# A ten-stage block kernel: work at the stage boundaries moved token tile by token tile

## The chip, the cores and the metric

The kernel runs on one core of a Trainium2 chip as one launch. The metric is the device time of one execution in microseconds (us), as the median of the runs made; lower is better. Names of engines as the profile has them: PE is the tensor engine's matmul stream, PEld its weight loads, DVE the vector engine, ACT the scalar engine, POOL GpSimd, SP the engine whose queue issues the DMAs.

## The reference, cut to what matters

256 tokens of width 1024 pass through two layers of a first block (a mixer of four branches, then a feed-forward network) and two layers of a second block (a mixer, an attention over 256 memory tokens, then a dense feed-forward network in layer 0 and eight experts with top 2 in layer 1). Every stage has the same skeleton:

```python
h = rms_norm(x, gain)
...
x = x + rms_norm(f @ w_out, gain_post)
```

In the first block the stage's output is normed before it is added; in the second it is added plainly (`x = x + f @ w_out`). All is float32. `h` feeds the next projections, all of them with K = 1024: `h @ w_in` and the like.

## The kernel before

Ten stages run one after the other: mix1, ffn1, mix1, ffn1, mix2, mem, ffn2 (dense), mix2, mem, ffn2 (`moe`). `xt` holds x as two token tiles of 128 rows, each in two halves of 512 columns. A float32 product is made of three matmuls in float32r (`mm3`, L310 to L312): each operand is split into a high part and a rest, so that a weight tile costs an ACT copy (L297) and a DVE subtraction (L298) after its DMA, all in `wload`. `wload` has 3 buffers for what the DMA brings (`wraw`, 512 KB each) and 4 for the split weights (`wsp`).

A stage ends with `as_1024` (L481): token-major `x @ W`, granule after granule of 128 rows of W, into four PSUM banks `po[t][n]`. The last granules (`TM` = 3 of 8 for mix1, `TF` = 4 of 22 for the ffns) have split weights of their own and are gone through bank by bank: all of token tile 0's two banks, then those of tile 1. What is left of the update of x is put in `pend` by `post_norm` (first block) or `add_x` (second block).

The next stage begins with `norm_T` (L364). It runs the pending update and the norm in the order of a string: `p` squares an output half, `g` multiplies by the gain, `r` makes the scale of the row (a DVE add, a POOL power), `u` updates x, `q` squares it, `s` makes the scale, `n` scales the row into `xn`; the digits are token tile and half. For this stretch the order of ACT and DVE is the one written out (`manual_schedule`); elsewhere a planner orders the instructions of an engine, and puts them where its model of times finds them ready. Then PE makes 16 transposes of `xn`, and ACT (`hh`, L333) and DVE (`hl`, L334) split the eight feature tiles, both token tiles together, with the gain column applied. `late` holds back the fourth weight load of the next stage until that is done; the first three may go before. Only then does the first projection start: in the ffn with weights as the stationary operand and 256 tokens moving (`ws_bank`); in mix1 with `w1a`, in mix2 with `pk` (keys, 200 columns), then `pi` (index queries, 512 columns).

In mix2 the order of PE is written out. It is `pk`'s matmuls, `pi`'s, the transposes of `keys` (L1012 to L1016), `pq`'s, and so on:

```python
pk = as_512(A['w2k'][l], h, 2, 200, "pk2")
pi = as_512(A['w2i'][l], h, 4, 512, "pq2")
keys(pk)
pq = as_512(A['w2q'][l], h, 4, 512, "pq2")
```

`keys` takes the two banks of `pk` (one for each token tile) through an rms scale per head and the rotary turn on ACT, DVE and POOL, tile 0 and then tile 1, and then has PE transpose the result `kd`.

In mix1 a string `SC1` gives PE's order, one letter a step of a generator (`v` is the gate's projection and its gelu). `moe` begins with the router's matmuls on `hh`, `hl` (L1656); it also needs the normed rows token-major with the gain (`th`), which POOL makes by four products with a gain row (L1701).

Of the kernel before, what the change touches and what calls it, by code (L numbers as in the profile page):

```python
# [9 lines left out]
F32 = mybir.dt.float32  # L10
# [48 lines left out]
# ---------------------------------------------------------------- host layout  # L59
# [13 lines left out]
PFM_W = _o  # L73

# [63 lines left out]
def pack(inp):  # L138
    z = {k: np.asarray(v) for k, v in inp.items()}
    d = {}  # L140
# [18 lines left out]
    d['pfm'] = np.stack(pf)  # L159

    a1, c1, s1, g1, u1, v1, gt, uq, ukv, ob, ou, fi, fo = [[] for _ in range(13)]
    for l in range(2):
# [19 lines left out]
        fi.append(_ws(h, 128))  # L182
        fo.append(_as(z['w_ffn_out'][l], 1))
    for nme, v in (('w1a', a1), ('w1c', c1), ('w1s', s1), ('w1u', u1), ('w1v', v1), ('w1g', gt), ('wuq', uq),
                   ('wukv', ukv), ('wob', ob), ('wou', ou), ('wfi', fi), ('wfo', fo)):
        d[nme] = np.stack(v)
# [32 lines left out]
    d['wf2'] = _ws(np.stack([gw, uw], 2).reshape(1024, 5632), 128)  # L219
# [9 lines left out]
    d['ffn2row'] = z['norm_ffn_2'][1:2]  # L229
# [3 lines left out]
# ---------------------------------------------------------------- device  # L233
def build(tc, A, out, stages=None, dbg=None):
# [3 lines left out]
    with ctx:  # L238
        mk = lambda n, b, **k: ctx.enter_context(tc.tile_pool(name=n, bufs=b, **k))
        cp = mk("cp", 1)  # L240
        wraw = mk("wraw", 3)
        wsp = mk("wsp", 4)
        hp = mk("hp", 1)
        st = mk("st", 6)
        scr = mk("scr", 3)
# [19 lines left out]
        # ------------------------------------------------ constants  # L265
# [21 lines left out]
        # ------------------------------------------------ helpers  # L287
# [29 lines left out]
        def ws_tile(o, w, x, kt, nt=0):  # L317
            """o [128, 256] = W[:, nt]^T x; w = (h, l) [128, kt, n]."""
# [26 lines left out]
        def mean_rstd(s2):  # L345
            """s2: the mean square of a row in two parts."""
# [8 lines left out]
        def settle():  # L355
            """what is left of the last update of xt, where no norm of its rows follows at once."""
# [7 lines left out]
        def norm_T(xs, gcol, pl=None, name="h"):  # L364
            """feature-major rms-normalised rows of xs, in two float32r parts; token-major.
            A pending update of xs is made in step with it."""
            pl = pl or hp
            u = pend.pop() if pend else dict(step={}, order='q00 q01 s0 n00 n01 q10 q11 s1 n10 n11', xn=None, close=lambda: None)
            hh = pl.tile([128, 8, 256], F32R, name=name + "h", tag="hh")
            hl = pl.tile([128, 8, 256], F32R, name=name + "l", tag="hl")  # L370
            xn = u['xn'] or hp.tile([128, 2, 1024], F32, name="xn", tag="x8")
# [1481 lines left out]
```

## Time and profile before

| what | before |
|---|---|
| runs, us | 2417.47, 2415.18, 2412.37; median 2415.18 |
| profiled execution, span from first to last instruction | 2401.5 us |
| median of the runs less that span | 13.7 us |
| PE busy | 2298.4 us, 96% of the span |
| DVE, ACT, POOL busy | 72%, 53%, 8% |
| mean granted PE clock | 0.977 of full speed |
| DMA | 429 MB, mean 179 GB/s |

The profiled execution's own time is its span; what the runs show beyond it lies around the program. A matmul's listed duration overlaps the next one's, so the cost of a stream is read from the distance of its starts, not from durations. Idle time of an engine that nothing waits for costs nothing.

### The profile page before, as it was taken

The page shows a single profiled execution, that of the slowest core. Times are in us where ns is not written, and L with a number is a line of the kernel's source. Part 1 is how long each engine was busy: PE and PEld are TensorE (multiplying, and loading weights), DVE is VectorE, ACT ScalarE, POOL GpSimd, SP SyncE. Part 2 cuts the span into 40 slices and gives each one's busy share as a digit, 9 for nine tenths or more (in the row PEclk, how much of TensorE's full clock was granted, in tenths as well). Part 3 has the DMA queues.
Part 4 walks back from the last instruction along what each step waited for, and adds up shares of the span by engine and source line. Part 5 has one row for each costly group of instructions (what it writes and reads, how often), then busy time and mean ns, then how long its engine had stood idle before and what let it go on. Part 6 is the DMA issues. An engine that isn't in the chain of part 4 may idle for free.

```text
span 2401.5 us, 39006 instructions
## 1 busy us (share of the span) xinstructions
PE 2298.4 (96%) x15116; PEld 2060.5 (86%) x15116; DVE 1732.2 (72%) x2879; ACT 1274.9 (53%) x1991; POOL 185.2 (8%) x179
## 2 busy tenths in 40 slices
PE   7999999999999999999999999999999979999998
PEld 7999989979999899787798799888788768888886
DVE  7987665559967655586946655477865768999987
ACT  5544454445544544456324554456432657777775
POOL 0100200001001100001111100001111110000000
PEclk9999999999999999999989999999998989999999
DMA  6455655645456565643214445553212548888986
GB/s 203 132 160 177 180 174 183 185 153 167 143 174 185 165 185 178 191 136 125 75 43 144 146 151 184 190 171 114 96 45 83 198 158 287 321 321 322 345 326 234
DMA packets 123218, 429.24 MB, mean 179 GB/s; under 512 B 14189, under 2 KB 15213, under 8 KB 123025
## 3 DMA queue, kind: packets, MB, share of 16 engines
q1 hardware_dynamic: 123024, 426.68, 54.6%
q8 instruction: 120, 1.97, 0.3%
q14 instruction: 74, 0.60, 0.1%
HBM read 425.57 MB, written 1.05 MB: 178 GB/s over the span
## 4 chain that ended last, share of the span: by engine, by line
PE 75%; DVE 9%; ACT 4%; DMA 3%; POOL 2%; issue 2%; POOLq 0%; ACTq 0%; DVEq 0%
PE pf L311 5%; PE pf L312 5%; PE pf L310 5%; PE pg L310 4%; PE pg L311 4%; PE pg L312 4%; PE po L312 3%; PE po L310 3%; PE po L311 3%; PE pgu L311 3%; PE pgu L312 3%; PE pgu L310 3%; DVE wl L298 2%; PE py L310 1%; PE pb L310 1%
## 5 line engine op out<-in xcount | busy, mean ns | idle before, releaser
L298 DVE TENSOR_TENSOR wl<-raw,wh 128x1024 fp32r<-128x1024 f32 (+2 forms) x788 | 947.7, 1214 | 323.5 <-ACT wh L297 315.3
L297 ACT ACTIVATE wh<-raw 128x1024 fp32r<-128x1024 f32 (+2 forms) x788 | 807.0, 1031 | 609.1 <-PE pg L311 137.5
L311 PE MATMUL pf<-hl,wh 128*128 128x256 f32 x1056 | 299.4, 284 | 0.3
L312 PE MATMUL pf<-hh,wl 128*128 128x256 f32 x1056 | 298.8, 283 | 0.0
L310 PE MATMUL pf<-hh,wh 128*128 128x256 f32 x1056 | 298.7, 284 | 0.0
L310 PE MATMUL pg<-hh,wh 128*128 128x256 f32 x768 | 225.6, 294 | 0.1
L312 PE MATMUL pg<-hh,wl 128*128 128x256 f32 x768 | 220.4, 287 | 1.0 <-DVE wl L298 1.0
L311 PE MATMUL pg<-hl,wh 128*128 128x256 f32 x768 | 220.4, 287 | 0.0
L311 PEld LDWEIGHTS pf<-hl,wh 128*128 128x128 f32 x1056 | 202.7, 192 | 1.3 <-DVE hl L334 1.3
L312 PEld LDWEIGHTS pf<-hh,wl 128*128 128x128 f32 x1056 | 202.7, 192 | 0.0
L310 PEld LDWEIGHTS pf<-hh,wh 128*128 128x128 f32 x1056 | 202.5, 192 | 0.2
L310 PEld LDWEIGHTS pg<-hh,wh 128*128 128x128 f32 x768 | 150.8, 196 | 4.9 <-issue 3.7
L311 PEld LDWEIGHTS pg<-hl,wh 128*128 128x128 f32 x768 | 150.9, 196 | 1.1 <-issue 1.0
L312 PEld LDWEIGHTS pg<-hh,wl 128*128 128x128 f32 x768 | 150.5, 196 | 1.4 <-DVE wl L298 1.4
L311 PE MATMUL pgu<-wl,heh 128*128 128x512 f32 (+1 forms) x384 | 145.3, 378 | 2.0 <-DVE wl L298 2.0
L312 PE MATMUL pgu<-wh,hel 128*128 128x512 f32 (+1 forms) x384 | 144.1, 375 | 0.0
L310 PE MATMUL pgu<-wh,heh 128*128 128x512 f32 (+1 forms) x384 | 143.4, 376 | 0.0
L566 DVE SCALAR_TENSOR_TENSOR yc<-z,htap,yc 128x256 f32<-128x256 f32 x240 | 110.7, 487 | 2.3
L310 PE MATMUL po<-wh,fh 128*128 128x512 f32 x216 | 85.7, 397 | 0.0
L311 PE MATMUL po<-wl,fh 128*128 128x512 f32 x216 | 85.4, 395 | 0.0
L312 PE MATMUL po<-wh,fl 128*128 128x512 f32 x216 | 85.4, 395 | 0.0
L311 PEld LDWEIGHTS pgu<-wl,heh 128*128 128x128 f32 x384 | 72.5, 189 | 13.9 <-DVE wl L298 3.1
(678 smaller groups left out, 5254.3 us busy)
## 6 DMA issues: line engine op xcount, KB each, us to landing
raw<-in_xg_dram SPq DMA_DIRECT2D x128, 512.0 KB, 5.4
raw<-in_wfi_dram SPq DMA_DIRECT2D x88, 512.0 KB, 3.6
raw<-in_xd_dram SPq DMA_DIRECT2D x88, 512.0 KB, 5.2
raw<-in_w1g_dram SPq DMA_DIRECT2D x64, 512.0 KB, 3.6
raw<-in_xg_dram SPq DMA_DIRECT2D x64, 384.0 KB, 4.6
raw<-in_wfo_dram SPq DMA_DIRECT2D x44, 512.0 KB, 3.7
raw<-in_wf_dram SPq DMA_DIRECT2D x44, 512.0 KB, 3.6
raw<-in_wob_dram SPq DMA_DIRECT2D x32, 512.0 KB, 3.7
```

The source lines that it names most:

```text
L297: act.activation(h[:, :n], r[:, :n], AF.Copy)
L298: dve.tensor_tensor(l[:, :n], r[:, :n], h[:, :n].bitcast(F32), op=OP.subtract)
L310: pe.matmul(o, a[0], b[0], start=first, stop=False)
L311: pe.matmul(o, a[0], b[1], start=False, stop=False)
L312: pe.matmul(o, a[1], b[0], start=False, stop=last)
L566: bg.append(lambda z=z, f=f, tap=tap, k=k: dve.scalar_tensor_tensor(yc[:, f], z[:, k:k + 256], tap, yc[:, f], op0=OP.mult, op1=OP.add))
```

## The change

What it does, in ten parts.

- The tails of `as_1024` become longer: `TF` 4 to 6, `TM` 3 to 5. In mix1 the split weights of the tail take tiles that are free by then.
- `norm_T` stays for the memory tokens; for x it is replaced by `norm_x`. The gain is a row, loaded one stage ahead (`gload`), and multiplied in with the scale: `n` is now a SCALAR_TENSOR_TENSOR. The order strings go on through the transposes (`T`), the high parts (`h`), the rests (`l`) and a first projection (`F`), each for one token tile, and PE is in the written order too. With no update pending (`ONEW`) only PE's order is written.
- `head` loads four granules of a 512-column weight ahead of the norm, so before its ACT and DVE steps, and gives `F`: 24 matmuls of 512 columns for one token tile, tokens stationary.
- What `F` is: in mix1 `v`'s projection, in the three dense ffns the first 512 columns (two gate and two up tiles; then 4 transposes bring the result feature-major), in mix2 `pi`. `mem` and `moe` have no `F`.
- In mix2 `pi` therefore goes ahead of `pk`, and nothing stands between `pk` and `keys` any more.
- `late` now holds back the first weight load behind the head's (the fourth for `mem` and `moe`).
- `SC1` is changed: `v` first, and the `u` steps earlier.
- `moe` takes `th` straight from `xn`; POOL's four products and the row's load are gone. `th` now lies in the buffers of `hh` and `hl`.
- `mh` of mix1 moves to other buffers; the pools are allocated from both ends of SBUF.
- Comments and docstrings are gone.

```diff
-OPOST = 'p00 g00 p01 g01 r0 p10 g10 p11 u00 q00 r1 u01 g11 q01 u10 q10 s0 u11 q11 n00 n01 s1 n10 n11'
-OADD = 'u00 q00 u01 q01 s0 u10 q10 n00 u11 n01 q11 s1 n10 n11'
-TF, TM, TE = 4, 3, 4
+OPOST = ('p00 g00 p01 r0 g01 u00 q00 u01 q01 g10 s0 p10 n00 n01 T0 h00 l00 p11 r1 h01 l01 g11 F0 '
+         'u10 q10 u11 q11 s1 n10 n11 T1 h10 l10 h11 l11 F1')
+OADD = ('u00 q00 u01 q01 s0 u10 n00 n01 T0 h00 l00 h01 l01 F0 '
+        'q10 u11 q11 s1 n10 n11 T1 h10 l10 h11 l11 F1')
+ONEW = 'q00 q01 s0 n00 n01 T0 h00 l00 h01 l01 F0 q10 q11 s1 n10 n11 T1 h10 l10 h11 l11 F1'
+TF, TM, TE = 6, 5, 4
-SC1 = ('ccckcchhchhhhhhvxvxvvacssassaxxssasassaassusuuuurggguggagggg'
+SC1 = ('vccckcchhchhhhhsxsxssacssassaxxuuasuauuaassusrgggggagggg'
...
+        def gload(l, n):
+            gains.append(cp.tile([128, 1024], F32, name="gn", tag="gn"))
+            nc.sync.dma_start(gains[-1], A['gnorm'][l, GN.index(n):GN.index(n) + 1].to_broadcast([128, 1024]))
+        def norm_x(first=None, free=0):
...
+            def scale(t, n):
+                dve.scalar_tensor_tensor(xn[:, t, HALF[n]], xt[:, t, HALF[n]], rs[t], gn[:, HALF[n]], op0=OP.mult, op1=OP.mult)
+            def turn(t):
+                for n in range(2):
+                    p = pT[t, n] = psum("pT")
+                    for k in range(4):
+                        c = slice(k * 128, (k + 1) * 128)
+                        pe.transpose(p[:, c], xn[:, t, n * 512 + k * 128:n * 512 + (k + 1) * 128], ident)
...
+            def high(t, n):
+                ins['a'] = act.activation(part(hh, t, n), quad(pT[t, n]), AF.Copy)
+            def low(t, n):
+                ins['d'] = dve.tensor_tensor(part(hl, t, n), quad(pT[t, n]), part(hh, t, n).bitcast(F32), op=OP.subtract)
+            step = dict(u['step'], q=square, s=stat, n=scale, T=turn, h=high, l=low,
+                        F=(lambda t: first(t, (hh, hl))) if first else lambda t: None)
+            with tc.manual_schedule(engines={E_.Activation, E_.DVE, E_.PE} if u['step'] else {E_.PE}):
+                for c_ in u['order'].split():
+                    step[c_[0]](*map(int, c_[1:]))
...
+            if u['step']:
+                late.extend([None] * free + [(ins['a'].ins, ins['d'].ins)])
+        def head(srcs, n, kt, nm):
+            ws = [sub3(wload(src, kt * n), kt) for src in srcs]
+            pz = []
+            def part(t, h):
+                pz.append(pmm(nm)[:, :n])
+                c = slice(t * 128, (t + 1) * 128)
+                for k in range(8):
+                    w = ws[k // kt]
+                    mm3(pz[t], (h[0][:, k, c], h[1][:, k, c]), (w[0][:, k % kt], w[1][:, k % kt]), k == 0, k == 7)
+            return part, pz
...
         def mix1(l):
-            h = norm_T(xt, G(l, 'mixpre'))
+            fv, pzv = head([A['w1v'][l, g] for g in range(4)], 512, 2, "pgv")
+            h = norm_x(fv)
...
-        def ffn_core(wi, wo, h, nt):
+        def ffn_core(wa, wi, wo, nt, ahead):
+            ff, pz = head([wa[g] for g in range(4)], 512, 2, "pfa")
+            h = norm_x(ff)
...
         def mix2(l):
-            h = norm_T(xt, G(l, 'mix2'))
+            fi_, pi = head([A['w2i'][l, g] for g in range(4)], 512, 2, "pq2")
+            h = norm_x(fi_)
...
                 pk = as_512(A['w2k'][l], h, 2, 200, "pk2")
-                pi = as_512(A['w2i'][l], h, 4, 512, "pq2")
                 keys(pk)
                 pq = as_512(A['w2q'][l], h, 4, 512, "pq2")
...
-                moe(h)
+                moe(norm_x(free=3))
...
-                th = [xp.tile([128, 2, 1024], F32R, name="th" + c_) for c_ in "hl"]
+                th = [hp.tile([128, 2, 1024], F32R, name="th" + c_, tag="h" + c_) for c_ in "hl"]
...
-                        pool.tensor_tensor(d, d, grow[:, ns], op=OP.mult)
```

## Rows read from the trace of the kernel before

**Rows 1.** Page, part 1: engine busy us, share of the span, instructions.

```profile
PE 2298.4 (96%) x15116; PEld 2060.5 (86%) x15116; DVE 1732.2 (72%) x2879; ACT 1274.9 (53%) x1991; POOL 185.2 (8%) x179
```

**Rows 2.** PE's waits, whole span: who waited for whom, us, times, longest.

```profile
PE pT L393 <- DVE pn L383: 20.1, 5, 5.2
PE pT L393 <- DVE xn L383: 14.1, 9, 7.8
...
PE pS L633 <- DVE yal L332: 3.1, 2, 1.6
```

**Rows 3.** PE's timeline, first mix1 to ffn1: start, duration, instruction, idle before.

```profile
313.83 0.40 PE L311 MATMUL po<-wtl,mh 128*128 128x512 f32 x1
314.07 0.40 PE L312 MATMUL po<-wth,ml 128*128 128x512 f32 x1
319.66 3.70 PE L393 MATMUL pT<-cst,pn 128*128 128x128 f32 x16 [5.20 <-DVE pn L383]
```

**Rows 4.** Windows, that ffn's `pf` matmuls alone: busy, count, clock, DMA.

```profile
322.00:336.00 14.00, 12.94 (x104) 0.95 0.35 114
322.00:340.00 18.00, 16.94 (x137) 0.96 0.45 130
```

**Rows 5.** Windows of PE at two boundaries: busy (count), granted clock, DMA share, GB/s.

```profile
316.00:318.00 2.00, 0.00 (x0) 0.63 0.08 31
322.00:323.00 1.00, 1.00 (x7) 0.50 0.00 0
323.00:324.00 1.00, 1.00 (x9) 0.83 0.00 0
1580.00:1582.00 2.00, 2.00 (x12) 0.50 0.49 107
```

**Rows 6.** Groups by form, 291 to 340 us: steps of the norm (busy, mean ns).

```profile
L350 POOL TENSOR_TENSOR r<-v,mhalf 128x1 f32<-128x1 f32 x4 | 3.0, 745 | 19.1 <-DVE v L348 19.1
L465 DVE SCALAR_TENSOR_TENSOR xt<-pn,r,xt 128x512 f32<-128x512 f32 x4 | 3.0, 744 | 0.1
L458 DVE TENSOR_TENSOR pn<-po,grow 128x512 f32<-128x512 f32 x4 | 2.6, 681 | 0.0
```

**Rows 7.** ACT's timeline in the tail of the first ffn1: the weight splits.

```profile
489.90 1.06 ACT L297 ACTIVATE wh<-raw 128x1024 fp32r<-128x1024 f32 x1 [1.74 <-PE po L312]
490.93 1.06 ACT L297 ACTIVATE wth<-raw 128x1024 fp32r<-128x1024 f32 x1
493.93 1.06 ACT L297 ACTIVATE wth<-raw 128x1024 fp32r<-128x1024 f32 x1 [1.94 <-DMA raw<-in_wfo_dram]
```

**Rows 8.** Timeline, first mix2: `pk`'s last matmul, the chain of `keys`, its transposes.

```profile
1028.63 0.28 PE L312 MATMUL pk<-wh,hl 128*128 128x200 f32 x1
...
1031.99 0.23 DVE L1009 COPY kd<-kd 128x128 f32<-128x128 f32 x1
...
1035.37 1.22 DVE L298 TENSOR_TENSOR wl<-raw,wh 128x1024 fp32r<-128x1024 f32 x1
...
1036.89 0.23 DVE L1009 COPY kd<-kd 128x128 f32<-128x128 f32 x1
...
1039.68 0.60 PE L1015 MATMUL pT<-cst,kd 128*128 128x128 f32 x4
```

**Rows 9.** PE's waits, mem to ffn2 (1350 to 1420), ffn2 to mix2 (1560 to 1620).

```profile
PE pT L393 <- DVE xn L383: 1.9, 3, 1.2
...
PE pT L393 <- DVE xn L383: 2.0, 2, 1.2
```

**Rows 10.** PE's timeline, beginning of `moe`.

```profile
1945.76 1.09 PE L393 MATMUL pT<-cst,xn 128*128 128x128 f32 x8 [1.18 <-DVE xn L383]
1948.46 0.39 PE L1656 MATMUL plT<-hh,w 128*16 128x256 f32 x1 [1.60 <-DVE hl L334]
...
1957.51 0.58 PE L1707 MATMUL pps<-sel,cst 128*128 128x16 f32 x2 [4.58 <-DVE w L1689]
```

**Rows 11.** PE's timeline, first stage: its first projection.

```profile
12.47 0.62 PE L310 MATMUL pz<-wh,hh 128*128 128x272 f32 x2
```

More of the change, by code (lines that the diff above doesn't have):

```diff
@@ L159, in pack @@
     d['pfm'] = np.stack(pf)
-    a1, c1, s1, g1, u1, v1, gt, uq, ukv, ob, ou, fi, fo = [[] for _ in range(13)]
+    d['gnorm'] = np.stack([z[n] for n in GN], 1)
+    a1, c1, s1, g1, u1, v1, gt, uq, ukv, ob, ou, fi, fo, fa = [[] for _ in range(14)]
+    first = lambda w: _as(w[:, :512].reshape(1024, 2, 2, 128).transpose(0, 2, 1, 3).reshape(1024, 512), 2)
     for l in range(2):
@@ L362, in settle, with norm_T @@
                 u['close']()
-        def norm_T(xs, gcol, pl=None, name="h"):
-            pl = pl or hp
-            u = pend.pop() if pend else dict(step={}, order='q00 q01 s0 n00 n01 q10 q11 s1 n10 n11', xn=None, close=lambda: None)
+        def norm_T(xs, gcol, pl, name):
             hh = pl.tile([128, 8, 256], F32R, name=name + "h", tag="hh")
             hl = pl.tile([128, 8, 256], F32R, name=name + "l", tag="hl")
+            xn = hp.tile([128, 2, 1024], F32, name="xn", tag="x8")
+            s2 = [tiny(2, "s2") for t in range(2)]
+            for t in range(2):
+                for n in range(2):
+                    d = scr.tile([128, 512], F32, name="sq", tag="s512")
+                    act.activation(d, xs[:, t, HALF[n]], AF.Square, scale=1.0 / 32, accum_out=s2[t][:, n:n + 1])
+                r = mean_rstd(s2[t])
+                for n in range(2):
+                    dve.tensor_scalar(xn[:, t, HALF[n]], xs[:, t, HALF[n]], r, None, op0=OP.mult)
+            ps_ = [bank2("pT") for k2 in range(4)]
+            with tc.manual_schedule(engines={mybir.EngineType.PE}):
+                for k in range(8):
+                    for t in range(2):
+                        pe.transpose(ps_[k // 2][:, k % 2, t * 128:(t + 1) * 128], xn[:, t, k * 128:(k + 1) * 128], ident)
+            for k in range(8):
+                split(hh[:, k], hl[:, k], ps_[k // 2][:, k % 2], gcol[:, k:k + 1])
+            return hh, hl
@@ new lines, in build @@
+        gains = []
+        def gload(l, n):
+            gains.append(cp.tile([128, 1024], F32, name="gn", tag="gn"))
+            nc.sync.dma_start(gains[-1], A['gnorm'][l, GN.index(n):GN.index(n) + 1].to_broadcast([128, 1024]))
+        def norm_x(first=None, free=0):
+            u = pend.pop() if pend else dict(step={}, order=ONEW, xn=None, close=lambda: None)
+            gn = gains.pop()
+            hh = hp.tile([128, 8, 256], F32R, name="hh", tag="hh")
+            hl = hp.tile([128, 8, 256], F32R, name="hl", tag="hl")
@@ L382, in scale @@
             def scale(t, n):
-                ins['d'] = dve.tensor_scalar(xn[:, t, HALF[n]], xs[:, t, HALF[n]], rs[t], None, op0=OP.mult)
-            step = dict(u['step'], q=square, s=stat, n=scale)
-            with (tc.manual_schedule(engines={mybir.EngineType.Activation, mybir.EngineType.DVE}) if u['step'] else ExitStack()):
+                dve.scalar_tensor_tensor(xn[:, t, HALF[n]], xt[:, t, HALF[n]], rs[t], gn[:, HALF[n]], op0=OP.mult, op1=OP.mult)
+            def turn(t):
+                for n in range(2):
+                    p = pT[t, n] = psum("pT")
+                    for k in range(4):
+                        c = slice(k * 128, (k + 1) * 128)
+                        pe.transpose(p[:, c], xn[:, t, n * 512 + k * 128:n * 512 + (k + 1) * 128], ident)
@@ L387, in norm_T @@
+            E_ = mybir.EngineType
+            with tc.manual_schedule(engines={E_.Activation, E_.DVE, E_.PE} if u['step'] else {E_.PE}):
                 for c_ in u['order'].split():
                     step[c_[0]](*map(int, c_[1:]))
-            u['close']()
-            ps_ = [bank2("pT") for k2 in range(4)]
-            with tc.manual_schedule(engines={mybir.EngineType.PE}):
-                for t, k in sorted(((t, k) for t in range(2) for k in range(8)), key=(lambda v: 0) if u['step'] else (lambda v: v[1] // 2)):
-                        pe.transpose(ps_[k // 2][:, k % 2, t * 128:(t + 1) * 128], xn[:, t, k * 128:(k + 1) * 128], ident)
@@ L394, in norm_T @@
-            for k2, p in enumerate(ps_):
-                for i in range(2):
-                    k = 2 * k2 + i
-                    a_, d_ = split(hh[:, k], hl[:, k], p[:, i], gcol[:, k:k + 1])
-                    if k == 7:
-                        late.extend([None] * 3 + [(a_.ins, d_.ins)] if u['step'] else ())
-            lasts[:] = a_.ins, d_.ins
-            return hh, hl, xn
+                    if c_ == 'n11':
+                        u['close']()
+            if u['step']:
+                late.extend([None] * free + [(ins['a'].ins, ins['d'].ins)])
@@ L1566, in mem @@
                     pk = as_512(A['wmk'][l, 0], mh)
-                    h = norm_T(xt, G(l, 'mem2'))
+                    h = norm_x(free=3)
+                    gload(l, 'norm_ffn_2')
                     pq = as_512(A['wmq'][l], h, tail=2)
```

118 lines of the change are left out of this document (67 added, 51 removed).

## The prediction

> **What bounds the kernel now.** I read the engines' shares first. PE is busy 96% of the span and no other engine over 72% [rows 1], so time can only come out of PE's own stream: its 103 us of idle time, and stretches in which it runs at a lower clock. The view of waits says where the idle time lies: 34.2 us stand before the transposes of the norm, 20.1 of it in five waits for the scaled rows of a post-normed stage (four of about 5 us, one small), 14.1 in nine waits elsewhere, of which 7.8 is the start of the program [rows 2]. Then PE's timeline at one boundary. The last `po` matmul starts at 314.07; starts there are 0.23 to 0.24 apart, so the product is through at 314.3. The transposes begin at 319.66, after 5.20 idle, and take 3.70 [rows 3]. The ffn's matmuls run 0.121 us apart (33 in 4 us), and 104 of them have begun by 336.0 [rows 4]: that stream stands as if it had started at 323.4. The boundary costs PE 323.4 - 314.3 = 9.1 us, and this, not the 5.2 of idle time, is what a better boundary can eat into. The clock is the rest: it is granted at 0.63 in 316 to 318, at 0.50 (the 1.2 GHz level) still in 322 to 323, and rises within 323 to 324 [rows 5]. So PE worked some 3.7 us (319.66 to about 323.3) at half speed, which lost 1.8.
>
> **The four boundaries behind a post-norm** (into both ffn1, the second mix1, the first mix2). Removed: the string in which tile 0's update stands behind tile 1's squares. Put in: tile 0 as far as its projection, then tile 1. Steps last 0.68 to 0.74 on DVE and 0.75 on POOL [rows 6]. `F0` is 24 matmuls of 512 columns, 24 x 0.235 = 5.6 us. Piece by piece, for PE, from the end of `po`:
> - 16 transposes, at the 1.09 us for eight that `moe` shows [rows 10], less their overlap: 2.0.
> - `T0`'s wait. In a six-granule tail tile 0's banks are done 8.4 us ahead (two banks of 18 x 0.235), and its chain (square, scale, update, square, scale, `n`) is eight to nine steps of 0.7 to 0.8, some side by side, 6 to 7 us. So 0 if it starts at once. But the head's four weight loads stand ahead of the norm. In the tail of before, splits started at 489.90, 490.93 and 493.93, the last after a wait for its DMA [rows 7]: 2.0 us a load. Loads are free of the four `wsp` buffers four granules ahead of the tail, 28 us before the end, and then come one more granule, six tail granules and four of the head: 11 x 2.0 plus 2.3 for the last split is 24, which leaves some 4 us before the end of `po` where the chain needs 6. Between 0 and 2, I take 1.5.
> - The first high part and rest of tile 0, less the other half's transposes under them: 0.85.
> - `T1`'s wait. While `F0` runs, DVE has two rests, `g11`, two updates and `n10` (six times 0.72), POOL two scales, and ACT's square stands between: about 8.5 us from the beginning of `T0`, and `F0` is through at 7.2. With the second half, 1.6.
> - Tile 1's parts: 0.35.
>
> The sum is 6.3, a saving of 2.8 each, 11.2 for four. The bounds are 4.8 a boundary (no first wait), a saving of 17.2, and 8.1 (the clock falls, below), 4.0.
>
> What of the clock there? The row says that 16 transposes from 319.66 on did not raise it; it rose among the projection's matmuls [rows 3, 5]. And in the second mix2 it stood at 0.50 from 1580 to 1582 [rows 5], though the two waits at that boundary are 2.0 us in all and its transposes had run between them [rows 9]. I take it that `F0`, 5.6 us of matmuls between the two groups of transposes, holds it up. The Trainium skill (TensorE: Matmul & The Clock Gate, Part 4: PE-mode transpose) says that a transpose does not count as PE activity in the way a matmul does; the traces agree. By that rule a stretch of waits and transposes alone counts as idle, and the clock could fall at each `T`: the third rival.
>
> **The two boundaries with a plain add and an `F`** (into the dense ffn2, the second mix2). They wait 1.9 and 2.0 [rows 9], the second with a slow clock. `T1`'s chain now lies under `F0`, but parts and rests of both tiles stay exposed. I take 1 and 2, together 3; bounds 0 and 5.
>
> **Keys in mix2, twice.** This is what the change uncovers. In before, `pk`'s last matmul starts at 1028.63, the first tile's `kd` is done at 1032.22, the second's at 1037.12, and PE transposes at 1039.68, behind `pi`'s 96 matmuls [rows 8]: the chain was hidden by 2.6 us to spare. `pi` is now ahead of `pk`, PE's order there is written out, and what is queued behind the four transposes is all of `pq`. So PE waits out the chain: 8.4 us as it stands. One weight split of 1.22 lies inside [rows 8] that may have been done earlier: 7.2. A wait of that length lowered the clock at the boundary above, and the restart at half speed lost 1.8 there [rows 3, 5]: 9.0, twice 18.0. Bounds: 2 x 3.6 = 7.2 if the second tile goes side by side with the first and the clock holds; 2 x 10.2 = 20.4 with nothing taken out. I stay near the upper end, since the row is the same chain on the same engines.
>
> **The start of `moe`.** It has no `F`, yet takes the string of tiles: tile 1's last update now stands on DVE behind tile 0's two rests, which wait for `T0` and the high parts. In before the second transposes began at 1945.76 and the router at 1948.46 [rows 10]; with two rests, an update, a square, a scale and `n` in line behind tile 0's transposes I put both 3 to 4 us later. The router needs both tiles. POOL's products vanish, but PE's wait of 4.58 behind the router ends with DVE's choice of experts [rows 10], so I count nothing for them; `th` must now wait for the router, as it lies in its operands' buffers. A loss of 3.5; bounds 0 and 5.
>
> **The start of the program.** Its first projection began at 12.47 [rows 11]. Four 512 KB granules and the gain's row now come first: a loss of 1, between a gain of 1 and a loss of 3.
>
> **At nothing.** The ffn's head is 48 x 0.235 = 11.3 us for 96 x 0.121 = 11.6, and gives the 0.3 back in four transposes. The gains' rows load a stage ahead, under hundreds of matmuls; without that cover `n` would wait about as long as the 1.94 in [rows 7]. `SC1` exchanges pieces of one length as cover of the attention; what PE waits there is 3.1 in two waits [rows 2], so 3 either way. Behind `F1` the next weights need a `wsp` buffer, the first of which falls free after 6 of `F1`'s 24 matmuls; the split's 2.3 us fit under the rest. Pools and buffers move no instruction.
>
> **Sum.** -11.2 - 3 + 18.0 + 3.5 + 1 = +8.3, so 2409.8 for the span of 2401.5. The runs' median stands 13.7 above that span, which I keep: 2423.5.
>
> **Rivals.**
> 1. The keys do not hold PE up, and the kernel gets faster: 2423.5 - 18.0 = 2405.5. For it: no row of before shows such a wait. Against: PE kept the written order there when `kd` was ready 2.6 us early [rows 8]. It decides if the two waits cost under 4.9 together (18.0 - 8.3 - 4.8), 2.4 each, which is less than the first tile's chain alone. I give 0.20.
> 2. The boundaries save all they can: the norm's steps go ahead of the late loads, so `T0` does not wait. 4 x 1.5 = 6 less: 2417.5, which a measurement can't tell from no change. For it: the planner mixes loads and steps where its times say so. Against: in before too three loads went ahead of the norm. 0.22.
> 3. The clock falls at the four boundaries all the same, 4 x 1.8 = 7.2 more: 2430.7. For it: the second mix2's row with short waits; against: `F0`. 0.13. The skill's sentence above would have it so.
> 4. The forecast, boundaries partly eaten by late weights, keys uncovered: 0.45.
>
> **How the numbers follow.** A change of 0.2%, 4.8 us, is about what measuring this kernel can tell from none. Rival 1 is faster: 0.20. Rival 2 lies within, and so does the forecast's lower edge: 0.22 + 0.05 = 0.27. The rest of the forecast and rival 3 are slower: 0.40 + 0.13 = 0.53. The range reaches from rival 1 to a little above rival 3, 2405 to 2434; outside lie the keys hidden with whole boundaries, and late weights, slow clock and the upper bound of the keys together. The forecast's own range is 2419 to 2428.
>
> **What would show it.** In the trace after: a wait of 6 to 9 us before the transposes of `kd` in both mix2, with a clock of 0.50 behind it; four boundaries with first waits under 2.5 us where 5 stood, and at most 7 us from the end of `po` to the end of `F1` beyond its 11.3 us of matmuls; the router of `moe` 3 us later after the last `po`; ACT's head splits ending about 4 us before the end of `po`. The prediction is wrong if the keys' wait is under 3 us, or if the boundaries cost 3 us or 9.

## The result, and the profile after

The changed kernel takes 2433.39 us (median; 2429.4 to 2434.1), the kernel before on the same chip 2413.77: a ratio of 1.0081, 95% interval 1.0057 to 1.0105. That is 0.8% or 19.6 us slower, where the prediction had 2423.5: just inside the upper end of its range (2434), and above the forecast's own 2419 to 2428.

The page of the kernel after, part 1, and its view of PE's waits over the whole span (who waited for whom; us in all, times, longest):

```profile
PE 2305.4 (95%) x14984; PEld 2056.3 (85%) x14984; DVE 1738.7 (72%) x2836; ACT 1267.2 (52%) x1948; POOL 175.3 (7%) x175
```

```profile
PE pT L430 <- DVE xn L423: 16.6, 4, 10.7
PE pT L681 <- DVE kr L678: 9.0, 2, 4.9
PE pT L430 <- DVE pn L423: 8.0, 5, 3.1
PE pT L1097 <- DVE v L349: 7.0, 2, 3.5
PE pT L1097 <- DVE kd L1091: 6.3, 2, 3.3
PE pT L606 <- DVE cn L598: 5.8, 2, 3.3
...
PE pz L323 <- DVE hl L439: 4.5, 3, 2.1
```

Against [rows 2]: the wait for `pn`, 20.1 us at the post-normed boundaries, is down to 8.0. What came in its place stands in four lines that the view of before does not have at this size: `kr` (L681) and `cn` (L606), the transposes of two short chains inside mix1 (the rotary part of the keys, and a small projection behind its rms norm), and twice L1097, the transposes of the keys in mix2. PE's busy time is about that of [rows 1].

Where the time went is read best by stage. The table gives the distance from the start of one stage's last `po` matmul to that of the next (PE's timeline; the first from the span's start, the last to its end), and so splits the difference of the two spans, 2431.0 - 2401.5 = 29.5:

| stage | before | after | difference | forecast |
|---|---|---|---|---|
| mix1, first | 314.1 | 326.1 | +12.0 | +1 |
| ffn1, two | 197.5, 197.4 | 193.9, 194.5 | -3.6, -2.9 | -2.8 each |
| mix1, second | 305.1 | 310.8 | +5.7 | -2.8 |
| mix2, first | 301.9 | 312.5 | +10.6 | +6.2 |
| mem, two | 66.5, 66.8 | 69.8, 69.0 | +3.3, +2.3 | 0 |
| ffn2, dense | 193.4 | 190.4 | -3.0 | -1.5 |
| mix2, second | 299.5 | 307.1 | +7.6 | +7.5 |
| moe | 459.3 | 456.9 | -2.4 | +3.5 |

The two ffn1 gained what was forecast, the dense ffn2 twice that. Of the 21 us that the whole lost beyond the forecast, the two mix1 hold 19.5, and the other stages nearly cancel. How far one profile can be trusted for a stage is said with the experiments and at the end.

**A boundary.** PE's and ACT's timelines of the kernel after, first mix1 to ffn1 (start, duration, instruction, idle before; `L519` is the square of an output half, `L308` the high part of a weight):

```profile
326.05 0.40 PE L323 MATMUL po<-wth,ml 128*128 128x512 f32 x1
329.50 1.97 PE L430 MATMUL pT<-cst,pn 128*128 128x128 f32 x8 [3.05 <-DVE pn L423]
```

```profile
318.63 0.57 ACT L519 ACTIVATE sq<-po 128x512 f32<-128x512 f32 x1
...
322.45 1.06 ACT L308 ACTIVATE wh<-raw 128x1024 fp32r<-128x1024 f32 x1 [1.92 <-DMA raw<-in_wfa_dram]
323.41 0.58 ACT L519 ACTIVATE sq<-po 128x512 f32<-128x512 f32 x1
```

Matmuls are 0.233 apart and tile 1's two banks take 30 of them, so both banks of tile 0 are complete at 326.3 - 7.0 = 319.3. Their second square could start then. It starts at 323.41, right behind the split of the head's fourth weight granule, which waited for its DMA. The four microseconds lost on ACT turn up as PE's 3.05.

By PE's timeline the four post-normed boundaries cost 7.3, 5.1, 7.3 and 4.3 us, counted as the prediction counts them, from the end of `po` to the end of `F1` less 11.3 us of matmuls.

**The keys.** PE's timeline in the first mix2, from `pk`'s last matmul to `pq`'s first, and the windows behind it (stretch, length, busy and count of PE, PEld, DVE, ACT, POOL, granted clock, DMA share, GB/s):

```profile
1046.36 0.28 PE L323 MATMUL pk<-wh,hl 128*128 128x200 f32 x1
1050.12 0.66 PE L1097 MATMUL pT<-cst,kd 128*128 128x128 f32 x2 [3.48 <-DVE v L349]
1053.83 0.69 PE L1097 MATMUL pT<-cst,kd 128*128 128x128 f32 x2 [3.05 <-DVE kd L1091]
1054.17 0.78 PE L321 MATMUL pq<-wh,hh 128*128 128x512 f32 x1
```

```profile
1049.40:1059.60 10.20, 6.43 (x17) 4.91 (x18) 6.97 (x21) 1.45 (x3) 1.66 (x1) 0.50 0.27 86
1059.80:1067.80 8.00, 8.00 (x36) 6.45 (x35) 3.83 (x4) 3.10 (x3) 0.00 (x0) 1.00 0.43 128
```

PE starts on `pq` 7.8 us after `pk`'s last matmul started. The granted clock is 0.50, the 1.2 GHz level, from 1049.4 to 1059.6, inside the wait and behind it. In [rows 8] the transposes stood behind `pi` and cost no wait.

**Inside mix1.** PE and DVE of the kernel after in the second mix1: `kr`'s transposes, and what DVE did ahead of its last copy.

```profile
553.56 0.44 PE L606 MATMUL pT<-cst,cn 128*128 128x128 f32 x2 [2.48 <-DVE cn L598]
...
566.58 0.66 PE L681 MATMUL pT<-cst,kr 128*128 128x128 f32 x2 [4.13 <-DVE kr L678]
```

```profile
561.26 0.55 DVE L758 TENSOR_SCALAR vn<-vn,ba,r 128x512 f32<-128x512 f32 x1 [1.70 <-POOL r L351]
561.72 0.18 DVE L671 TENSOR_TENSOR m<-kr,TB 128x32 f32<-128x32 f32 x1
...
563.22 1.21 DVE L309 TENSOR_TENSOR wl<-raw,wh 128x1024 fp32r<-128x1024 f32 x1
...
566.22 0.35 DVE L678 COPY kr<-kro 128x128 f32<-128x128 f32 x2
```

DVE stood 1.70 us at the last step of `v`'s layer norm, which waited for POOL. The first step of the rotary turn of `kr` is right behind it. PE waits for the end of that chain. Half clock falls here too: 564.6 to 571.4, in and behind this wait, at a granted clock of 0.50. In all 13.7 us of each mix1 ran at half clock, where before it was 3.4 in the first and 6.8 in the second.

### The profile page after: what moved, and what is told of

It is laid out like the page before. It is cut to its first block, busy times and chain, and to the rows that moved or that the text cites. A ratio compares the mean times of both kernels' runs of the same rounds, so it can differ in the third digit from the quotient of the medians.

```text
span 2431.0 us, 38664 instructions
## 1 busy us (share of the span) xinstructions
PE 2305.4 (95%) x14984; PEld 2056.3 (85%) x14984; DVE 1738.7 (72%) x2836; ACT 1267.2 (52%) x1948; POOL 175.3 (7%) x175
## 5 line engine op out<-in xcount | busy, mean ns | idle before, releaser
L309 DVE TENSOR_TENSOR wl<-raw,wh 128x1024 fp32r<-128x1024 f32 (+2 forms) x778 | 936.4, 1215 | 339.9 <-ACT wh L308 330.0
L308 ACT ACTIVATE wh<-raw 128x1024 fp32r<-128x1024 f32 (+2 forms) x778 | 799.4, 1032 | 663.2 <-PE pg L322 147.0
L321 PE MATMUL pf<-hh,wh 128*128 128x256 f32 x960 | 270.7, 282 | 0.0
L323 PE MATMUL pf<-hh,wl 128*128 128x256 f32 x960 | 270.5, 282 | 0.0
L322 PE MATMUL pf<-hl,wh 128*128 128x256 f32 x960 | 270.3, 282 | 0.0
L322 PEld LDWEIGHTS pf<-hl,wh 128*128 128x128 f32 x960 | 180.9, 188 | 0.1
L321 PEld LDWEIGHTS pf<-hh,wh 128*128 128x128 f32 x960 | 180.9, 188 | 0.1
L323 PEld LDWEIGHTS pf<-hh,wl 128*128 128x128 f32 x960 | 180.8, 188 | 0.0
L321 PEld LDWEIGHTS pgu<-wh,heh 128*128 128x128 f32 x384 | 72.3, 188 | 10.1
L323 PEld LDWEIGHTS pgu<-wh,hel 128*128 128x128 f32 x384 | 72.2, 188 | 9.5
L321 PE MATMUL po<-wh,fh 128*128 128x512 f32 x192 | 75.1, 391 | 0.0
```

The costliest lines, as they stand in the source:

```text
L308: act.activation(h[:, :n], r[:, :n], AF.Copy)
L309: dve.tensor_tensor(l[:, :n], r[:, :n], h[:, :n].bitcast(F32), op=OP.subtract)
L321: pe.matmul(o, a[0], b[0], start=first, stop=False)
L322: pe.matmul(o, a[0], b[1], start=False, stop=False)
L323: pe.matmul(o, a[1], b[0], start=False, stop=last)
```

## The experiments

Each ratio is against the kernel before, run on the same chip; 0.001 is 2.4 us, and the changed kernel stands at 1.0081. Line numbers shift a little from kernel to kernel. The difference of two ratios carries both intervals: an estimate from their widths is some 7 us either way in the last column (9 for `tails43`). So the losses and gains of 10 and more are clear of zero, and 3 and 5 are not.

| kernel | ratio, 95% interval | against the changed kernel |
|---|---|---|
| k_cover | 1.0030 (1.0013 to 1.0046) | -12 us |
| b_pi_first | 1.0095 (1.0073 to 1.0117) | (+23 us against before) |
| k_nof | 1.0038 (1.0023 to 1.0053) | -10 |
| v_undo | 1.0028 (1.0010 to 1.0045) | -13 |
| v_late | 1.0030 (1.0016 to 1.0044) | -12 |
| v_bank | 1.0060 (1.0039 to 1.0081) | -5 |
| w_last | 1.0040 (1.0024 to 1.0055) | -10 |
| tails43 | 1.0124 (1.0097 to 1.0151) | +10 |
| nof_old | 1.0068 (1.0046 to 1.0089) | -3 |
| all_late | 0.9918 (0.9895 to 0.9940) | -39 |
| all_mix | 0.9868 (0.9845 to 0.9891) | -51 |
| all_start | 0.9900 (0.9879 to 0.9920) | -44 |

### The keys: b_pi_first, k_cover, k_nof

The exchange alone, in the kernel before:

```diff
-                pk = as_512(A['w2k'][l], h, 2, 200, "pk2")
                 pi = as_512(A['w2i'][l], h, 4, 512, "pq2")
+                pk = as_512(A['w2k'][l], h, 2, 200, "pk2")
                 keys(pk)
```

> The kernel before with two lines exchanged: pi's projection ahead of pk's, so that keys follow pk at once. Theory (this exchange alone uncovers the keys, whatever the boundaries do): two waits of 6 to 7 us and a slower clock behind each, 13 to 20 us slower than before: 2427 to 2434. Rival (the wait belongs to the new start of the stage, in which late weights and splits delay the chain): under 5 us slower than before.

Measured: 2435.08 us, 22.9 more than before (17.6 to 28.2): above the expected range, which the interval still reaches. PE's timeline of the first mix2 of this kernel:

```profile
1041.20 0.27 PE L312 MATMUL pk<-wh,hl 128*128 128x200 f32 x1
1044.61 0.41 PE L1015 MATMUL pT<-cst,kd 128*128 128x128 f32 x2 [3.14 <-issue]
1048.26 0.69 PE L1015 MATMUL pT<-cst,kd 128*128 128x128 f32 x2 [3.23 <-DVE kd L1009]
```

The same 6.4 us of waiting without any other part of the change: it is the order of two projections, not the new start of the stage.

The changed kernel with `pq` put over the chain:

```diff
-                keys(pk)
-                pq = as_512(A['w2q'][l], h, 4, 512, "pq2")
+                kd = keys(pk)
+                pq = as_512(A['w2q'][l], h, 4, 512, pz=[psum("pq2") for t in range(2)])
+                keys_T(kd)
```

> The changed kernel with one thing else: in both mix2 the matmuls of pq stand between the chain of keys and its four transposes (pq in two banks of the other PSUM pool). Theory (the keys' chain is uncovered, and its wait slows the clock): the two waits for v and kd of 6.5 and 6.8 us go, and most of the 17 us at half clock that stand behind them, which cost up to 8.5: 13 to 22 us less than the changed kernel, so 2411 to 2420 where it takes 2433. Rival (the chain ends a little before something else that is as late, and its wait turns up at the transposes of the queries): each mix2 shorter by under 3 us, 2428 to 2433.

Measured: 2420.43, 12 us less. Both hold in part. The waits for `kd` are gone, and half of their time (3.25 and 3.13) is back at the transposes of the index queries:

```profile
1055.22 0.60 PE L1100 MATMUL pT<-cst,kd 128*128 128x128 f32 x4
1055.65 0.60 PE L1122 MATMUL pT<-cst,ro 128*128 128x128 f32 x4
1059.50 1.09 PE L1122 MATMUL pT<-cst,ro 128*128 128x128 f32 x4 [3.25 <-DVE ro L1114]
```

`ro` needs only `pi`, which was through before `pk` began; the queries stand behind the keys in the program, and with the order turned round in the kernels with four repairs (below) no such wait is left. In this kernel's one profile the first mix2 is 11.3 us shorter than in the changed kernel's and the second 3.5 longer, with 44.4 us at half clock against 30.7; the runs carry the verdict.

The changed kernel with the projections at mix2's beginning in the order of before (the norm stays token tile by token tile):

```diff
-            fi_, pi = head([A['w2i'][l, g] for g in range(4)], 512, 2, "pq2")
-            h = norm_x(fi_)
+            h = norm_x(free=3)
...
                 pk = as_512(A['w2k'][l], h, 2, 200, "pk2")
+                pi = as_512(A['w2i'][l], h, 4, 512, "pq2")
```

> The changed kernel with mix2's beginning as before: no projection in the norm, then pk, pi, keys, pq. Theory (keys lie under pi's 96 matmuls again): both waits of 6.5 to 6.8 us and the slow clock behind them go, 17 to 22 us, and the two boundaries lose the projection that lay under tile 1's chain, 2 to 4 us each: 10 to 17 us less than the changed kernel, 2416 to 2423. Rival (the projection in the norm is worth as much there as the keys cost): within 4 us of the changed kernel.

Measured: 2423.69, 10 us less, at the edge of the theory's range. No wait at the keys' transposes is left among the longer ones, but the waits at the two boundaries into mix2 are 5.3 and 3.4, where the changed kernel has 0.4 and none. In its one profile mix2 is only 3.0 and 0.4 us shorter than in the changed kernel's: 47.8 and 41.0 us of it ran at half clock, 51.2 and 30.7 in the changed kernel and 34.1 and 27.3 before (see the end). The runs carry the verdict here, not that profile.

### `v` first in mix1: v_undo, v_late, v_bank

Mix1's projections and string as before, in the changed kernel (its norm stays token tile by token tile):

```diff
-SC1 = ('vccckcchhchhhhhhsxsxssacssassaxxuuasuauuaassusrgggggagggg'
+SC1 = ('ccckcchhchhhhhhvxvxvvacssassaxxssasassaassusuuuurggguggagggg'
-            fv, pzv = head([A['w1v'][l, g] for g in range(4)], 512, 2, "pgv")
-            h = norm_x(fv)
+            h = norm_x(free=3)
...
             def gate_v():
+                pzv = [pmm("pgv") for t in range(2)]
+                for g in range(4):
+                    w = sub3(wload(A['w1v'][l, g], 1024), 2)
...
```

> The changed kernel with mix1 as before: no projection in the norm, v's projection at its old letters, the old string SC1. Theory (gelu and layer norm of v, now first in the stage, stand on ACT and DVE ahead of the chains of cn and kr): the waits for cn and kr, 8.2 us in the first mix1 and 6.6 in the second, go, with 10 us at half clock that stand behind them; the boundary into the second mix1 loses what lies under its first projection, 2 to 3 us: mix1 shorter by 8 to 12 us in layer 0 and 5 to 8 in layer 1, 13 to 20 us less than the changed kernel, 2413 to 2420. Rival (the stalls of mix1 come from the pools and buffers that moved, or from the longer tail, and not from v): under 4 us less.

Measured: 2419.40, 13 us less. The first mix1 is 316.8 us long (-9.2), the second 307.4 (-3.4). In its view of waits `cn` is at 2.7 and `kr` at 0.7:

```profile
PE pT L605 <- DVE cn L597: 2.7, 2, 2.1
PE pT L680 <- DVE kr L677: 0.7, 1, 0.7
```

Only the letter moved, and the two banks with it; the `u` steps stay early:

```diff
-SC1 = ('vccckcchhchhhhhhsxsxssacssassaxxuuasuauuaassusrgggggagggg'
+SC1 = ('ccckcchhchhhhhhvsxsxssacssassaxxuuasuauuaassusrgggggagggg'
...
-                pz.append(pmm(nm)[:, :n])
+                pz.append((psum if nm == "pgv" else pmm)(nm)[:, :n])
```

> The changed kernel with the letter v of SC1 moved behind the sixth h of the run of six (so that gelu and layer norm of v come where they came before), and v's two banks taken from the other PSUM pool, since they are held until then; its projection stays in the norm. Theory (order of ACT and DVE): the waits for cn and kr go as when v is undone, and the boundaries keep their gain: 13 to 22 us less than the changed kernel, 2411 to 2420, and at most the time of the kernel in which v is undone. Rival (the projection in the norm itself is what delays cn and kr, by its weights' splits and its banks): the waits stay, under 5 us less.

Measured: 2419.80, 12 us less, as much as undoing the whole. The second mix1 falls to 303.6 (-7.3), below before; the first only to 323.1 (-2.9), and that is within the scatter: in the kernels here whose first mix1 is that of the changed kernel it is 323.4 to 326.1 long. Of the 14.8 us that PE waits at these two groups of transposes, 9.1 stay:

```profile
PE pT L606 <- DVE v L349: 5.3, 2, 3.0
...
PE pT L681 <- DVE kr L678: 3.8, 2, 2.6
```

In the first mix1 what is left before `cn` is another thing queued ahead of it: on ACT in this kernel a split of the next weight, which waits for its DMA, stands ahead of the squares of `cn`.

```profile
42.03 1.06 ACT L308 ACTIVATE wh<-raw 128x1024 fp32r<-128x1024 f32 x1 [1.68 <-DMA raw<-in_w1c_dram]
43.00 0.36 ACT L596 ACTIVATE cn<-pz 128x256 f32<-128x256 f32 x1
```

The banks alone (the second hunk of v_late):

> The changed kernel with v's two banks taken from the other PSUM pool, and nothing else; gelu and layer norm of v stay first in the stage. Rival of the theory of the order (the second pz waits for a bank that gelu holds): the waits for cn, kr and pz of mix1 go as in the kernel with v late, 8 to 14 us less than the changed kernel. Theory (order of ACT and DVE, not banks): kr's waits of 4 to 5 us stay, only pz's 1.3 goes: 0 to 4 us less, 2429 to 2433.

Measured: 2425.91, 5 us less (the intervals of this and of the changed kernel overlap). Most of the waits of the theory stay; the 1.3 of the second `pz` is gone, so that one was for a bank:

```profile
PE pT L681 <- DVE kr L678: 7.8, 2, 4.3
PE pT L606 <- DVE cn L598: 5.5, 2, 3.0
```

So the order of ACT and DVE is what holds `kr` up: it falls to 3.8 only when the letter moves too, and to 0.7 in `v_undo`. For `cn` that is not shown. Its transposes wait 5.3 with the letter moved; in the first mix1 this goes (0.6) only where the projection leaves the norm, in `v_undo`, and in the second it is 2.1 even there. By the runs 5 of the 12 us come with the banks and 7 with the letter; these shares lie within the intervals and are not settled.

### Boundaries: w_last, tails43, nof_old

The fourth granule of the head behind tile 0's chain (a step `W` behind `n01`):

```diff
-            ws = [sub3(wload(src, kt * n), kt) for src in srcs]
+            ws = [sub3(wload(src, kt * n), kt) for src in srcs[:-1]]
+            def last():
+                ws.append(sub3(wload(srcs[-1], kt * n), kt))
...
-OPOST = ('p00 g00 p01 r0 g01 u00 q00 u01 q01 g10 s0 p10 n00 n01 T0 h00 ...
+OPOST = ('p00 g00 p01 r0 g01 u00 q00 u01 q01 g10 s0 p10 n00 n01 W T0 h00 ...
```

> The changed kernel with the last of the head's four granules loaded and split behind the step n01 of the order string, so behind tile 0's chain and not ahead of it. Theory (ACT stands in its order at that split, which waits for its DMA, with tile 0's second square behind it): the first waits of the four post-normed boundaries, 3.0, 1.3, 2.9 and 0.4, fall under 0.5 each, the projection then waits for its fourth weight under 0.5: 5 to 9 us less than the changed kernel, 2424 to 2428. Rival (tile 0's chain is that long by itself, or the fourth weight then comes too late for the projection): under 2 us less, or more time.

Measured: 2418.51, 10 us less. ACT at the same boundary of this kernel:

```profile
318.84 1.06 ACT L308 ACTIVATE wh<-raw 128x1024 fp32r<-128x1024 f32 x1 [0.58 <-DMA raw<-in_wfa_dram]
319.80 0.58 ACT L524 ACTIVATE sq<-po 128x512 f32<-128x512 f32 x1
...
324.65 1.05 ACT L308 ACTIVATE wh<-raw 128x1024 fp32r<-128x1024 f32 x1
```

The second square is at 319.80 and not at 323.41, and PE's first wait at this boundary is 0.25 instead of 3.05. Both ffn1 are 3.3 us shorter than in the changed kernel, and none of their time is at half clock. The Trainium skill (TensorE: Matmul & The Clock Gate, Part 1, Architectural detail) calls the queues of ACT and DVE strict first-in, first-out. The trace agrees: a square whose banks were full at 319.3 stood until 323.41 behind a split that waited for its data.

The old lengths, `TF, TM = 4, 3`:

> The changed kernel with the old lengths of the tails, TF 4 and TM 3. Theory (late weights, not the banks of tile 0, set when tile 0's chain runs): the chain starts at about the same time before the end of po, first waits longer by 0 to 1.5 us each: 0 to 6 us more than the changed kernel, 2433 to 2439. Rival (the longer tail is what the boundaries' gain rests on): the four boundaries and the ffn2 lose all that they gained, 10 to 14 us more, 2443 to 2447.

Measured: 2442.88, 10 us more: the time of the rival, though the intervals would allow the theory's too. The four boundaries cost 11.6, 7.0, 11.5 and 8.7 us where the changed kernel has 7.3, 5.1, 7.3 and 4.3, so the longer tail is what most of their gain rests on. The view of waits gives 20.1 us for `pn`, which is what [rows 2] has:

```profile
PE pT L430 <- DVE pn L423: 20.1, 4, 6.8
```

What it works through is nevertheless the late weights. ACT at the first boundary of this kernel, whose last `po` matmul starts at 323.93:

```profile
323.47 1.06 ACT L308 ACTIVATE wh<-raw 128x1024 fp32r<-128x1024 f32 x1 [1.73 <-DMA raw<-in_wfa_dram]
324.44 0.58 ACT L519 ACTIVATE sq<-po 128x512 f32<-128x512 f32 x1
```

The last split begins 0.5 us ahead of the last `po` matmul's start where it began 3.6 ahead with the longer tail (322.45 against 326.05). Each granule of the tail has split weights of its own; a longer tail lets the loads behind it come earlier. That it also completes tile 0's banks earlier does not come to bear while the split stands in the way. My expectation of 0 to 6 us had the mechanism and missed this link.

Another order where no projection stands between the tiles:

```diff
+ONOF = ('u00 q00 u01 q01 s0 u10 q10 n00 u11 n01 q11 s1 T0 n10 n11 T1 h00 l00 h10 l10 h01 l01 h11 l11')
...
-                for c_ in u['order'].split():
-                    step[c_[0]](*map(int, c_[1:]))
+                for c_ in (u['order'] if first else ONOF).split():
+                    if c_[0] in step:
+                        step[c_[0]](*map(int, c_[1:]))
```

> The changed kernel with another order for the stages that have no projection in the norm (both mem, and moe): both tiles' updates and scales ahead of the transposes, the parts in the order in which the next matmuls use them. Theory (the string by token tile is a loss there, as nothing lies between the tiles): moe's router begins 2 to 3 us earlier after the last po, the two waits of 2.1 for hl in mem shrink to 1: 4 to 6 us less than the changed kernel, 2427 to 2429. Rival (PE catches up behind the router, where it waits for the choice of experts anyway): under 1.5 us less.

Measured: 2429.30, 3 us less, with intervals that overlap: not settled. In its profile the router starts 7.6 us after the last `po` (1979.39 against 1971.79), where the changed kernel has 8.75; the expectation was 2 to 3 earlier. Mem hardly gains (69.4 and 67.7 long against 69.8 and 69.0), as no update is pending there and only PE's order is written.

### Together: all_late, all_mix, all_start

`all_late` has the fourth granule late, `v` late with its banks, the order of `nof_old`, and this in mix2:

```diff
+                queries(0, pi, iT2, None)
+                queries(1, pi, iT2, None)
-                keys(pk)
+                kd = keys(pk)
                 pq = as_512(A['w2q'][l], h, 4, 512, "pq2")
+                keys_T(kd)
-                queries(0, pi, iT2, None)
-                queries(1, pi, iT2, None)
```

> The changed kernel with four repairs at once: the last head granule behind n01, v's gelu at its late letter with its banks from the other pool, the order for the stages without a projection, and in mix2 another cover of the keys: after pk the index queries of pi, then keys' chain under pq, then keys' transposes. Theory (the losses are separate, and each comes back): about 10, 14, 3 and 13 to 20 us less than the changed kernel, together 34 to 45 with some overlap at the second mix1: 2390 to 2400, faster than before by 0.5 to 0.9%. Rival (they share one resource, the splits of ACT and DVE, or the slow clock of mix2 takes its part back): 2404 or more.

Measured: 2395.91, ratio 0.9918: 39 us less than the changed kernel and 20 less than before. That is what separate losses that add would give: 10, 12 and 3 from the runs above leave 14 for the keys, where `k_cover`, with another cover, gave 12.

`all_mix` is `all_late` with the projection in the norm and the string undone for layer 0's mix1 alone:

```diff
-            fv, pzv = head([A['w1v'][l, g] for g in range(4)], 512, 2, "pgv")
-            h = norm_x(fv)
+            if l:
+                fv, pzv = head([A['w1v'][l, g] for g in range(4)], 512, 2, "pgv")
+                h = norm_x(fv)
+            else:
+                h, pzv = norm_x(free=3), []
...
-                for c_ in SC1:
+                for c_ in (SC1 if l else SC0):
```

> As the kernel with four repairs, but the first mix1 (layer 0, where no output projection precedes) as before the change: no projection in its norm, the old string. Theory (at the program's start the head's weights and the gain's row delay the norm, and nothing is gained, as no chain is hidden): the first stage 5 to 8 us shorter than in the kernel with four repairs: 2384 to 2395. Rival (the loss at the start is the order of v alone): within 2 us of it.

Measured: 2382.39, ratio 0.9868 (0.9845 to 0.9891), 1.3% faster than before and below the expected range. The first stage is 6.5 us shorter than in `all_late` (315.5 against 321.9), where the runs differ by 13.5. In the two profiles the rest lies mainly in the two mix2, 3.9 and 3.8 us shorter with the same code and 13.6 us less at half clock; that part is not shown to come from the edit. PE's timeline of its first mix2 shows the keys covered:

```profile
1019.33 0.28 PE L326 MATMUL pk<-wh,hl 128*128 128x200 f32 x1
1019.44 1.03 PE L1145 MATMUL pT<-cst,ro 128*128 128x128 f32 x8
...
1031.28 0.39 PE L326 MATMUL pq<-wh,hl 128*128 128x512 f32 x1
1031.51 0.60 PE L1123 MATMUL pT<-cst,kd 128*128 128x128 f32 x4
```

and its waits at the transposes of `cn` (two lines), `kr` and `pn` are (5.8, 9.0 and 8.0 in the changed kernel)

```profile
PE pT L618 <- DVE v L352: 2.2, 1, 2.2
...
PE pT L693 <- DVE kr L690: 1.9, 2, 1.2
...
PE pT L433 <- DVE pn L426: 0.7, 3, 0.3
...
PE pT L618 <- DVE cn L610: 0.6, 1, 0.6
```

One thing more at the start:

```diff
-                h, pzv = norm_x(free=3), []
+                h, pzv = norm_T(xt, G(0, 'mixpre'), hp, 'h'), []
...
-        gload(0, 'norm_mix_pre')
```

> The kernel with four repairs and the old first mix1, with one thing more undone at the program's start: the first norm takes the gain as a column in the split of the feature tiles (as the norm of the memory tokens does), so that no gain row is loaded ahead of it. Theory (the scaled rows wait there for the DMA of the gain's row, and the first projection begins at 15.25 where it began at 12.47): 2 to 3 us less at the start, 2379 to 2381. Rival (the start is set by the transposes and the first weights, which are as late): under 0.7 us.

Measured: 2387.87, ratio 0.9900, its interval overlapping that of `all_mix`. The first projection does begin earlier, at 14.14 instead of 15.25, but the stage is 315.3 us long against 315.5. The gain is 1.1 at one place and none at the end of the stage: the expected 2 to 3 did not come. As 3.4 us of that stage ran at half clock here and none in `all_mix`, a gain of up to 1.7 may hide behind it.

## Why the prediction was right or wrong

**Direction and place of the main loss: right.** The keys wait 6.5 and 6.8 us where 7.2 was set, and half clock follows both. `b_pi_first` prices the two at 22.9 together (17.6 to 28.2), where the sum had 18.0 and its bound 20.4, both inside that interval. That the clock took more than the 1.8 each that I carried over from a boundary is shown for the first mix2: 10.2 us at half clock, PE busy in 6.43 of them, which lost up to 3.2. In the second it was 6.8 us, PE busy in 4.0: up to 2.0. Rival 1 is out.

**The post-normed boundaries: right in kind and in sum, and the sum partly by luck.** The four cost 24.1 us together, where 4 x 6.3 = 25.2 was set. But the pieces differ: `T1`'s wait, set at 1.6, is 0.1 to 0.4, and against it `T0`'s wait and the half clock behind it cost more than the 1.5 at the two boundaries out of mix1. I had taken a six-granule tail for all four; mix1's has five, so that tile 0's banks are done 7.0 us ahead and not 8.4. The first waits are 3.05, 1.3, 2.9 and 0.4 (the 3.05 and 2.9 behind the tails of five), and their cause is the one given, late weights ahead of tile 0's chain: `w_last` gets 10 us back, where rival 2 had 6 for the same thing. The last head split began 3.8 us before the end of `po` at the first boundary and ended 2.8 before it, where about 4 was said. Rival 3, the clock, came true at two of the four: both boundaries from mix1 into ffn1, with waits of 3, ran 3.4 us at half clock; the other two, with 1.3 and 0.4, did not. With the wait gone (`w_last`) none of it is left, though the same transposes run.

**The step that failed: "at nothing", `SC1`, 3 either way.** This term is mis-sized. It cost 12 to 13 us, some 7 either way, by `v_undo` (which takes the projection out of the norm as well) and `v_late` (which moves the banks as well). I had looked at the string as cover for PE, letter for letter, and not at what ACT and DVE do for the letter that was moved first: gelu, statistics and scale of `v`, ahead of `kr`; for `cn`, the projection in the norm and the splits that come with it count too, since its wait stayed when the letter moved. The boundary into the second mix1 did gain, but the stage lost 5.7 in all. It is the question that the forecast put to the keys (what is queued ahead of the chain, and who waits for that) left unasked three paragraphs on. In the first mix1 the row of ACT adds a second thing:

```profile
40.12 1.28 ACT L508 ACT_TABLE_LOAD   x1
41.41 0.79 ACT L508 ACTIVATE TB<-ang 128x704 f32<-128x704 f32 x1
42.23 1.28 ACT L745 ACT_TABLE_LOAD   x1
...
45.96 0.36 ACT L596 ACTIVATE cn<-pz 128x256 f32<-128x256 f32 x1
```

The tables' sine and gelu's tanh each load a function table, 1.28 us a time, and the squares of `cn`'s second half stand behind both. In the kernel before (35.13 and 37.36) and in `v_undo` (31.22 and 36.96) the two loads stand behind all squares of `cn`. The Trainium skill (ScalarE activation tables: per-element evaluation and per-set limits, What a function is on this engine) puts two functions of different sets one such load apart, 1283 ns; the trace agrees. No run here moves the tables alone.

**The start: mis-sized.** A loss of 1 was set, 3 at most. The scaled rows wait 1.94 us for the DMA of the gain's row, as this row of DVE in the kernel after shows:

```profile
9.94 2.74 DVE L423 SCALAR_TENSOR_TENSOR xn<-xt,r,gn 128x512 f32<-128x512 f32 x4 [1.94 <-DMA gn<-in_gnorm_dram]
```

With `v` late the first stage was still 9.0 longer than before. Between `all_late` and `all_mix` it falls by 6.5, to 1.4 above before: the projection in the norm, put where no output projection precedes it, costs about that much together with its string. Up to 5 of it can be the clock, as 10.2 us of the stage ran at half clock in `all_late` and none in `all_mix`; how much is the head's loads, or the slow first matmuls (0.43 us apart until 18.5, 0.23 after), was not taken apart.

**Moe and mem.** The router of moe begins 8.75 us after the last `po` where it began 6.27 after: +2.5 for a forecast of 3 to 4, by the way that was given, PE's wait of 4.65 for tile 1's rows. But the whole stage is 2.4 shorter than before. In the seven other kernels that have the changed moe as it is, it is 455.6 to 459.4 long, in one profile each, and 457.8 in the other kernel with the old one; so the stage's difference lies within its scatter, and this term is not settled. Mem, which I left out, lost 3.3 and 2.3: its projection now waits 2.1 for a rest (`hl`) where it waited 0.9, and in the first mem 3.4 us are at half clock.

**The sum against the median.** I added 13.7 us for what lies around the program. The profiled execution after took 2432.82 with a span of 2431.0, and all kernels here show 1.8 to 1.9. So the profile of before was of one of its shortest executions, and the 29.5 us between the two spans overstate the 19.6 between the medians. The step was wrong, and by luck brought the forecast 1.4 nearer (+8.3 on 2413.8 is 2422.1). What was missing beyond that is 11.3, about what mix1's order cost; that the time still fell inside the range is luck too, since the bound on that term was 3.

## What to carry to other kernels

When a step is moved to the front of a stage, follow each engine's own queue from there: what its vector and scalar work now stands ahead of, and which short chain PE needs first. A weight split that may have to wait for its DMA belongs behind the chain that PE waits for, not ahead of it, and a longer tail with weights of its own moves all later loads forward. Several losses of 10 us that hide a gain can be taken back one by one; here the change, without its part in the first stage, is worth 1.3% once its new waits are covered. What the four repairs would do without the change was not run.

## What the runs showed of the hardware

The same mix2 code takes different times by its clock. The second mix2 of the changed kernel and of `tails43`, whose code inside that stage is the same (they differ in the tail of the stage ahead of it; windows):

```profile
1598.20:1905.40 307.20, 287.24 (x2018) 246.52 (x2017) 213.28 (x501) 133.42 (x258) 42.17 (x29) 0.95 0.33 103
```

```profile
1600.20:1915.40 315.20, 295.65 (x2017) 254.34 (x2017) 214.36 (x503) 134.10 (x259) 41.08 (x29) 0.92 0.31 100
```

The numbers of instructions and PE's idle time (20.0 and 19.6) agree; the second is 8.0 us longer at a granted clock of 0.92 instead of 0.95. With 307.2 x 0.05 = 15.4 and 315.2 x 0.08 = 25.2, the time lost to the clock differs by 9.9, about all of it. What tips the clock there was not found. So a single profile of this kernel can't tell a change of some 8 us in mix2 from none, and the 29.5 between the two spans may hold such a part: its first mix2 has 51.2 us at half clock where before had 34.1, and only 10.2 of these lie at the keys.
